# A hybrid attention and ConvFFN step on one core: the last two output tiles projected together, and split operands kept in memory between passes

## The chip, the cores and the metric

One core of a Trainium2 chip runs the whole step as one program. The metric is device time in microseconds (us) of one execution. TensorE (PE) does matrix products, VectorE (DVE), ScalarE (ACT) and GpSimd (POOL) do the elementwise work, SyncE (SP) issues all large transfers in program order, and 16 DMA engines carry them between memory (DRAM) and the on-chip buffers.

## The reference

The parts that the change touches, after attention and gated linear attention have made the mixed rows:

```python
def _conv_ffn(h, hist, p):
    L = h.shape[1]
    a, g = jnp.split(h @ p['w_up'], 2, axis=-1)
    a_ext = jnp.concatenate([hist.astype(a.dtype), a], axis=1)
    conv = p['b_conv']
    for j in range(CONV_W):
        conv = conv + p['w_conv'][j] * a_ext[:, j:j + L]
    y = (jax.nn.gelu(conv) * g) @ p['w_down']
    return y, a_ext[:, L:]
# per layer: x1 = x + gate * (mixed @ w_o);  h = rms(x1) modulated;  y = x1 + gate2 * conv_ffn(h)
```

There are 2048 prompt rows and 64 sample rows of width 1024; the FFN is 2816 wide, and w_up has 2 x 2816 columns. All arrays are float32.

## The kernel before

**Splits.** A float32 product is made of three faster products: each operand is split into a rounded part ("hi", a cast on ACT, L88) and the rest ("lo", a subtraction on DVE or POOL, L91). The up-projection of the FFN is done by a 2 x 2 block scheme with seven products, numbered m = 1, 6, 2, 5, 3, 7, 4 in the order in which they run. It needs eight combinations of the normed rows (the tile `comb`: four are written by ACT and DVE when the rows come back from a transpose, L1098 and L1100, four are sums on POOL, L1102 to L1105) and seven of the weights (`sraw`, L1181, then `wu` hi and lo).

**The output stage.** The 2112 rows are 17 tiles: 0 to 15 of 128 prompt rows, and 16 of 64 sample rows. `out_tile` is a generator with the steps: load and transpose the mixed rows `mx` (L1064), split them (`mT`), 48 matmuls with `w_o` (L96), gate and add the residual (`x1`, L1078 and L1079), store `x1`, norm it, transpose it (L1091), make `comb`, and then either split `comb` into the operands `h2` of pass 0 (tiles 0 to 5) or store it (tiles 6 to 16, `comb_d`, L1112: eight slots of 4 x 64 numbers for each of 128 partitions, thus 4096 pieces of 256 bytes). The loop around it runs the steps of neighbouring tiles side by side. `comb` has one buffer, so the next tile's L1100 waits until the store has landed. A scheduler orders each engine's instructions, each engine then runs its list in that order.

**The ConvFFN.** Three passes over the rows (tiles 0 to 5, 6 to 11, 12 to 16), 22 slots each, one per block of 128 FFN columns. A slot's PE work is the seven up products (L1287) and, between them, the down products of the slot before (L1467). All else in a slot is put in order by hand-written event times (`at(t, fn)`). In the last slot of passes 0 and 1 the operands of the next pass are fetched from `comb_d` (L1439, one transfer per product) and split again, hi on ACT (L1442), lo on DVE or POOL (L1446). The finished rows of a pass are gated on DVE (L1500), added to `x1` on POOL or DVE (L1505) and stored. `fst` is the buffer into which `w_up` and `w_down` are loaded. `conv_rows` loads and transposes the convolution's weights and history (L1196).

Of the kernel before, what the change touches and what calls it, by code (L numbers as in the profile page):

```python
# [11 lines left out]
F32 = mybir.dt.float32  # L12
F32R = mybir.dt.float32r
# [8 lines left out]
P = 128  # L22
D = 1024
# [38 lines left out]
def kernel(  # L62
# [51 lines left out]
    comb_d = [dr.tile([P, 8, 4, 64 * nt + 32 * smp], F32, tag=f"combd{t}", name=f"comb_d{t}") for t, nt, smp in PASSES[1:]]  # L114
# [138 lines left out]
    def norm_rows(pool, x, n, bufs=1):  # L253

        junk = pool.tile([P, D], BF16, tag="junk", name="junk", bufs=1)
# [4 lines left out]
        xn = pool.tile([P, D], F32, tag="xn", name="xn", bufs=bufs)  # L260
        V.tensor_scalar(xn[:n], x[:n], r[:n], None, op0=ALU.mult)
        return xn
# [786 lines left out]

    def out_tile(t, n, seq, src, pos0, tok0):  # L1050
# [24 lines left out]
        x1 = wk.tile([P, D], F32, tag="x1", name="x1", bufs=1)  # L1075
# [6 lines left out]
        xn = norm_rows(wk, x1, n)  # L1082
# [84 lines left out]
    def load_cols(c0, pool=None, bufs=4):  # L1167
# [32 lines left out]
    w0 = c6.enter_context(tc.tile_pool(name="w0", bufs=1, side="right", reuse_waits="tile"))  # L1200
# [4 lines left out]
    for t in range(len(tiles)):  # L1205
        g = outs[t]
        prev = outs[t - 1] if t else iter(())
        nxt = outs[t + 1] if t + 1 < len(tiles) else iter(())
        next(nxt, None)
        next(g, None)  # L1210
        if t == 0:
            next(g)
# [4 lines left out]
        next(prev, None)  # L1217
        next(prev, None)
        if t == len(tiles) - 1:
            next(g)  # L1220
            c6a.close()
            c4.close()
            fw = c7.enter_context(tc.tile_pool(name="fw", bufs=1, reuse_waits="tile"))
            raws.append({"a": load_cols(P), "g": load_cols(FF + P)})
            for m in (5, 6, 7, 3):
                block_sum(raws[0], m)
            w_f = {}
            for m, s in PRODUCTS:
                w_f[m] = two(f"wu{m}_")
                split(*w_f[m], block(raws[0], m), lo_eng=G if m in (3, 5, 6, 7) else V)  # L1230
        next(nxt, None)
        next(prev, None)

    with ExitStack() as c8:
        wk = c8.enter_context(tc.tile_pool(name="wk5", bufs=1, reuse_waits="tile"))
        ac = None

        def open_acc():
            nonlocal ac
            c6.close()  # L1240
            ac = c8.enter_context(tc.tile_pool(name="ac", bufs=1, reuse_waits="tile"))
# [25 lines left out]
        def slot(n, base, w, raw, raw_next, behind):  # L1267
# [111 lines left out]
            at(max(end[7] + 2.8, end[3] + 5.7), gated, 1, "m5", G)  # L1379
            at(end[4] + .1, add_bank, "b7")  # L1380
# [52 lines left out]
            if last_f and p + 1 < len(PASSES):  # L1433
                w1 = 64 * PASSES[p + 1][1] + 32 * PASSES[p + 1][2]
                there = base
# [12 lines left out]
                for m, s in PRODUCTS:  # L1448
                    there = max(there, end[m]) + 3.3
                    at(end[m] + .1, fetch, m, s)  # L1450
                    for i in range(2):
                        ks, eng = slice(2 * i, 2 * i + 2), G if m in (5, 6, 7) else V
                        at(there + 1.5 + i, half_hi, m, ks)
                        at(there + 2.6 + (2.0 if eng is G else 1.2) * i, half_lo, m, ks, eng)

            def down_tile(i, t):
# [4 lines left out]
                def products():  # L1461
                    if first_f:
                        acc[i] = ac.tile([P, D], F32, tag="acc", name="acc", bufs=8)
# [15 lines left out]

                at(t, products)  # L1480
                t += 6 * .232
                at(t + .1, add)
                if last_f:
# [3 lines left out]

                    def residual(c):
                        if c == 0 and i == nt:
                            g2[:] = [gate_rows(ac, 1, 1, "acc", 8)]  # L1490
                        elif c == 0 and n + 1 == NF and i == 0:
                            g2[:] = [gate_rows(ac, 1, 0, "gate")]
                        o["gate", i] = g2[0]
                        o["xs", i, c] = x = ac.tile([P, 512], F32, tag="xs", name="xs", bufs=2)
                        Q.dma_start(x[:rows_], x1_d[tile_ * P:tile_ * P + rows_, c * 512:(c + 1) * 512])
# [6 lines left out]
                    def finish_(c):  # L1502
                        cc = slice(c * 512, (c + 1) * 512)
                        a = o["acc", i][:rows_, cc]
                        (V if last and i % 2 else G).tensor_tensor(a, a, o["xs", i, c][:rows_], op=ALU.add)  # L1505
                        Q.dma_start((y_sample if i == nt else y_prompt[tile_ * P:tile_ * P + rows_])[:, cc], a)

                    for c in range(2):
                        at(t - 1.5 + c * .5 if last else late - 4 + c, residual, c)
                        at(t + 1.4 + c * .1 if last else late + 2.5 * c, gate_, c)  # L1510
                        at(t + 2.5 + c * .1 if last else late + 1 + 2.5 * c, finish_, c)
# [8 lines left out]
        at(.1, next, outs[-1])  # L1520
        at(7.5, next, outs[-1])
        at(13.0, open_acc)

        def conv_state():
            for s, dst in ((0, conv_prompt), (1, conv_sample)):
                pt = bank()
                T.transpose(pt[:2 * NF, :P], cout[s].rearrange("p j f -> p (j f)"), ident)
                ob = wk.tile([P, 768], F32, tag="cv", name="ob")
# [61 lines left out]
def _arrays(inputs):  # L1590
    out = {}
    for n, a in inputs.items():
        a = np.ascontiguousarray(np.asarray(a))
        if n in ("c_prompt", "c_sample") or (a.ndim == 2 and n not in ("c_prompt", "c_sample")):
            out[n] = a
        elif n in ("cache_ckv", "cache_kpe", "state_gla", "state_ffn_conv"):
# [13 lines left out]
```

## Time and profile before

| | us |
|---|---|
| three runs, median (lowest to highest) | 3171.83 (3169.92 to 3175.9) |
| the profiled execution | 3175.5 |
| its span in the trace | 3173.6 |
| PE busy in it | 3028.5 |
| DVE busy in it | 2479.6 |
| ACT busy, POOL busy in it | 1472.2, 1439.5 |

The span is from the first to the last instruction. The trace's times below count from the span's start. Attention fills the span up to about 1439, the output stage runs to about 1664, the FFN to the end.

### The profile page before, as it was taken

The numbers are of one execution on the slowest core, as the hardware profiler recorded it, in microseconds if no ns is written. First come the engines' busy times: TensorE is split into PE (matmuls) and PEld (weight loads), VectorE is DVE, ScalarE is ACT, GpSimd is POOL, SyncE is SP. The second block draws the span as 40 slices with busy tenths as digits, with TensorE's granted clock in tenths as the row PEclk, the third lists the DMA queues.
The fourth block names the chain that finished last, engine by engine and source line by source line (L and its number), as shares of the span: only waits on it lengthen the run. The fifth ranks groups of instructions, "written<-read, shape, count | busy, mean of one in ns | idle before, by whom it ended". The sixth has DMA issues, their size and how long they took to land. (4 is left out here: it accounts for less than half of the span.)

```text
span 3173.6 us, 46762 instructions
## 1 busy us (share of the span) xinstructions
PE 3028.5 (95%) x16730; PEld 2650.4 (84%) x16730; DVE 2479.6 (78%) x4617; ACT 1472.2 (46%) x3188; POOL 1439.5 (45%) x1170
## 2 busy tenths in 40 slices
PE   7999899999989999999998999999999999899996
PEld 4999788788758888887877999998899999789995
DVE  4766678778678888875546778788878778999997
ACT  4655433333247777773334434334434434444442
POOL 0233222212132222202336666666866665888884
PEclk9999899999979999999998999999999999999998
DMA  7544521111121112103574222223322222533232
GB/s 256 152 134 124 153 70 62 56 51 54 34 84 50 56 48 65 38 21 118 159 193 110 69 71 61 80 60 132 118 78 63 73 68 64 161 100 94 80 90 77
DMA packets 327641, 287.67 MB, mean 91 GB/s; under 512 B 104503, under 2 KB 272263, under 8 KB 327407
## 3 DMA queue, kind: packets, MB, share of 16 engines
q1 hardware_dynamic: 327407, 284.67, 30.4%
q8 instruction: 132, 2.16, 0.3%
q14 instruction: 102, 0.84, 0.1%
HBM read 217.63 MB, written 66.98 MB: 90 GB/s over the span
## 5 line engine op out<-in xcount | busy, mean ns | idle before, releaser
L1287 PE MATMUL bank<-h,wu 128*128 128x384 f32 (+1 forms) x5544 | 951.9, 326 | 38.3 <-ACT m L1306 35.3
L1287 PEld LDWEIGHTS bank<-h,wu 128*128 128x128 f32 x5544 | 917.9, 190 | 68.6 <-ACT m L1306 41.0
L1467 PE MATMUL bank<-wd,u 128*128 128x512 f32 (+1 forms) x2244 | 571.6, 398 | 5.4 <-DVE wd L1359 3.6
L1359 POOL TENSOR_TENSOR wu<-sraw,wu 128x512 fp32r<-128x512 f32 x252 | 365.4, 1450 | 347.0 <-ACT wu L1415 347.0
L1467 PEld LDWEIGHTS bank<-wd,u 128*128 128x128 f32 (+1 forms) x2244 | 411.9, 187 | 91.6 <-DVE wd L1359 5.1
L1478 DVE TENSOR_TENSOR acc<-acc,bank 128x512 f32<-128x512 f32 (+1 forms) x714 | 451.2, 678 | 41.2 <-PE bank L1467 38.3
L96 PE MATMUL bank<-w_g,hs 128*128 128x512 f32 (+4 forms) x1632 | 319.7, 347 | 0.0
L1359 DVE TENSOR_TENSOR wu<-fst,wu 128x512 fp32r<-128x512 f32 x189 | 215.6, 1166 | 93.6 <-ACT wu L1415 92.0
L96 PEld LDWEIGHTS bank<-w_g,hs 128*128 128x128 f32 (+1 forms) x1632 | 249.9, 188 | 33.3 <-issue 2.7
L91 DVE TENSOR_TENSOR pp<-bank,pp 128x512 fp32r<-128x512 f32 (+5 forms) x344 | 196.0, 577 | 38.2 <-ACT pp L88 33.7
L876 PE MATMUL bank<-pp,vv 128*128 128x512 f32 (+5 forms) x688 | 210.0, 392 | 13.0 <-DVE ob L900 6.7
L1345 DVE SCALAR_TENSOR_TENSOR cv<-a_sb,fcol,cv 128x768 f32<-128x768 f32 (+1 forms) x132 | 216.5, 1640 | 3.8 <-ACT cv L1341 1.5
L851 ACT ACTIVATE pr<-bank,mx 128x512 f32<-128x512 f32 (+4 forms) x328 | 204.7, 629 | 30.5 <-DVE mx L844 21.1
L88 ACT CAST pp<-bank 128x512 fp32r<-128x512 f32 (+5 forms) x344 | 170.0, 504 | 100.0 <-PE bank L863 95.9
L839 DVE TENSOR_REDUCE mx<-bank 128x1 f32<-128x512 f32 (+4 forms) x328 | 194.9, 599 | 24.4 <-PE bank L838 18.4
L96 PE MATMUL bank<-w_o,mT 128*128 128x512 f32 (+1 forms) x816 | 198.4, 400 | 1.4 <-ACT mT L88 0.9
L1312 POOL TENSOR_TENSOR m<-m,m 128x384 f32<-128x384 f32 (+1 forms) x132 | 173.6, 1315 | 42.4 <-ACT m L1306 35.3
L1415 ACT CAST wu<-sraw 128x512 fp32r<-128x512 f32 x252 | 154.9, 615 | 80.9 <-PE bank L1287 47.3
L96 PEld LDWEIGHTS bank<-w_o,mT 128*128 128x128 f32 (+1 forms) x816 | 148.8, 185 | 44.2 <-DVE mT L91 6.1
L863 PE MATMUL bank<-ident,pr 128*128 128x128 f32 (+1 forms) x1112 | 179.2, 276 | 3.8 <-DVE pp L91 2.9
L1181 POOL TENSOR_TENSOR sraw<-fst 128x512 f32<-128x512 f32 x128 | 181.7, 1420 | 0.0
L863 PEld LDWEIGHTS bank<-ident,pr 128*128 128x128 f32 (+1 forms) x1112 | 135.9, 141 | 39.9 <-DVE pp L91 9.3
(254 smaller groups left out, 5142.3 us busy)
## 6 DMA issues: line engine op xcount, KB each, us to landing
fst<-w_up SPq DMA_DIRECT2D x128, 512.0 KB
fst<-w_down SPq DMA_DIRECT2D x64, 512.0 KB
x<-x_prompt SPq DMA_DIRECT2D x32, 512.0 KB
ada_w<-w_ada SPq DMA_DIRECT2D x64, 256.0 KB
comb_d<-comb SPq DMA_DIRECT2D x10, 1024.0 KB
wst<-w_ada SPq DMA_DIRECT2D x16, 512.0 KB
hT_d<-hT SPq DMA_DIRECT2D x16, 512.0 KB
hT<-hT_d SPq DMA_DIRECT2D x16, 512.0 KB
```

What stands on the lines that cost most here:

```text
L91: (lo_eng or V).tensor_tensor(lo, src, hi.bitcast(F32), op=ALU.subtract)
L96: T.matmul(out, a, b, start=first and i == 0, stop=last and i == 2)
L839: V.reduce_max(mx[:qn, c:c + 1], po[:qn, :b - a], axis=AX.X)
L851: S.activation(pr[:qn, :b - a], box["s", i, j][:qn, :b - a], AF.Exp, bias=nb, accum_out=ls[:qn, i, j:j + 1])
L863: T.transpose(pt[:kn, i * qn:(i + 1) * qn], pr[:qn, j * P - a:j * P - a + kn], ident[:qn, :qn])
L876: T.matmul(box["o"][:, cs_], vv[:kn, key0 // P + j, :], pp[i][:kn, cs_], start=j == 0 and i == 0, stop=j == nk - 1 and i == 1)
L1181: G.tensor_tensor(s, x, y, op=op)
L1287: T.matmul(b[:, :cols_], w[m][i][:, k], h2[m][j][:, k, :cols_], start=first and k + i + j == 0, stop=k == 3 and i == 1, skip_group_check=n ...
L1345: V.scalar_tensor_tensor(v, o["a"][:, j:j + tot], col(j), v, op0=ALU.mult, op1=ALU.add)
L1359: eng.tensor_tensor(out[1], src, out[0].bitcast(F32), op=ALU.subtract)
L1467: T.matmul(po[c][:rows_], o["u"][a][:, c0:c0 + rows_], o["wd"][b][:, c * 512:(c + 1) * 512], start=a + b == 0, stop=a == 1)
L1478: V.tensor_tensor(x, x, y, op=ALU.add)
```

## The change

1. `conv_rows` moves from tile 4 to before the first projection, and uses buffers of `xn` and `comb`.
2. Tiles 15 and 16 are projected together (`project`), with the loop over `k` outside, so that each piece of `w_o` serves both.
3. Tiles 6 to 16 split `comb` in the output stage, and store seven hi and seven lo parts in three transfers (28, 8 and 20 times 64 numbers per partition: 7168 pieces of 256 bytes). The later passes fetch both parts, 14 transfers, and split nothing.
4. The first slot's `w_up` is no longer loaded three tiles ahead into a pool of its own, but after the last projection's place in the program. The host stores `w_up` by column block, so that a partition's piece is 4 KB long and not 512 bytes.
5. In the last slot the residual rows are loaded early, whole rows at a time, into free `fst` and `acc` buffers; nine of the ten final additions go to POOL; the convolution's state is written within the slot.
6. Smaller: the norm writes its square into `xn`, `x1` has two buffers, the accumulators lie in two pools.

```diff
     def out_tile(t, n, seq, src, pos0, tok0):
...
-        po = [bank(), bank()]
-        for k in range(KD):
-            for c in range(2):
-                mm3(po[c][:n], [mT[i][:, k, :n] for i in range(2)],
-                    [w_o[k][i][:, c * 512:(c + 1) * 512] for i in range(2)], k == 0, k == KD - 1)
+        mTs[t] = mT, n
         yield "proj"
+        po = pos.pop(t)
...
-            Q.dma_start(comb_d[p - 1][:, :, :, c0:c0 + hn], comb[:, :, :, :hn])
+            hi = wk.tile([P, 7, 4, 64], F32R, tag="hi", name="hi", bufs=1)
+            for m, s in PRODUCTS:
+                h, l = hi[:, s - (s > 2), :, :hn], c_(s)
+                split(h, l, l, lo_eng=G if m in (4, 5, 6, 7) else V)
+            dst = comb_d[p - 1]
+            Q.dma_start(dst[:, 0, :, :, c0:c0 + hn], hi[:, :, :, :hn].bitcast(F32))
+            Q.dma_start(dst[:, 1, 0:2, :, c0:c0 + hn], comb[:, 0:2, :, :hn])
+            Q.dma_start(dst[:, 1, 2:7, :, c0:c0 + hn], comb[:, 3:8, :, :hn])
         yield "done"
...
+    def project(*ts):
+        for t in ts:
+            pos[t] = [bank(), bank()]
+        for k in range(KD):
+            for t in ts:
+                mT, n = mTs[t]
+                for c in range(2):
+                    mm3(pos[t][c][:n], [mT[i][:, k, :n] for i in range(2)],
+                        [w_o[k][i][:, c * 512:(c + 1) * 512] for i in range(2)], k == 0, k == KD - 1)
...
-        s = (pool or fw).tile([P, KD, P], F32, tag="fst", name="fst", bufs=bufs)
-        Q.dma_start(s, w_up[:, c0:c0 + P].rearrange("(k p) f -> p k f", p=P))
+        s = fw.tile([P, KD, P], F32, tag="fst", name="fst", bufs=4)
+        Q.dma_start(s, w_up[c0 // P])
...
     next(outs[0])
-        if t == 4:
-            conv_rows(w0)
-        if t == len(tiles) - 4:
-            raws = [{"a": load_cols(0, w0, 2), "g": load_cols(FF, w0, 2)}]
+    conv_rows(wk4b)
+    for t in range(len(tiles) - 1):
+        g, nxt = outs[t], outs[t + 1]
+        last = t == len(tiles) - 2
+        next(nxt)
+        next(g)
+        if last:
+            next(outs[t - 1])
+            next(outs[t - 1])
+            next(nxt)
+            next(nxt)
+            project(t, t + 1)
+            next(outs[t - 1])
+        else:
+            project(t)
...
+    raws = [{"a": load_cols(i * P), "g": load_cols(FF + i * P)} for i in range(2)]
...
                 def fetch(m, s):
                     moving(m)
-                    Q.dma_start(h2[m][1].bitcast(F32)[:, :, :w1], comb_d[p][:, s])
-                def half_hi(m, ks):
-                    S.copy(h2[m][0][:, ks, :w1], h2[m][1].bitcast(F32)[:, ks, :w1])
-                def half_lo(m, ks, eng):
-                    h, l = h2[m][0][:, ks, :w1], h2[m][1][:, ks, :w1]
-                    eng.tensor_tensor(l, l.bitcast(F32), h.bitcast(F32), op=ALU.subtract)
+                    for i in range(2):
+                        Q.dma_start(h2[m][i].bitcast(F32)[:, :, :w1], comb_d[p][:, i, s - (s > 2)])
...
                     def residual(c):
...
-                        o["xs", i, c] = x = ac.tile([P, 512], F32, tag="xs", name="xs", bufs=2)
-                        Q.dma_start(x[:rows_], x1_d[tile_ * P:tile_ * P + rows_, c * 512:(c + 1) * 512])
+                        if not last:
+                            o["xs", i, c] = x = ac[1].tile([P, 512], F32, tag="xs", name="xs", bufs=2)
+                            Q.dma_start(x[:rows_], src[:, c * 512:(c + 1) * 512])
+                        elif c == 0:
+                            x = fw.tile([P, D], F32, tag="fst", name="fst", bufs=4) if i < 3 else acc_tile()
+                            Q.dma_start(x[:rows_], src)
+                            o["xs", i, 0], o["xs", i, 1] = x[:, :512], x[:, 512:]
...
-                        (V if last and i % 2 else G).tensor_tensor(a, a, o["xs", i, c][:rows_], op=ALU.add)
+                        (V if last and i == nt and c else G).tensor_tensor(a, a, o["xs", i, c][:rows_], op=ALU.add)
...
-                        at(t - 1.5 + c * .5 if last else late - 4 + c, residual, c)
+                        at(base + 8.0 + i if last else late - 4 + c, residual, c)
...
-        at(.1, next, outs[-1])
-        at(7.5, next, outs[-1])
+        at(8.0, next, outs[-2])
+        at(15.5, next, outs[-2])
+        at(17.0, next, outs[-1])
+        at(27.0, next, outs[-1])
```

Three places in the order of the engines' instructions follow. The first is PE at the start of the output stage; `mx` is tile 0's mixed rows, `fr` and `fh` the convolution's rows. Before:

```order
L1064 MATMUL bank_16938<-ident_66,mx_16699 128x128 x4
L1064 MATMUL bank_16945<-ident_66,mx_16699 128x128 x4
L96 MATMUL bank_16954<-w_o0_0_9755,mT0_16936 128x512
L96 MATMUL bank_16954<-w_o1_0_9756,mT0_16936 128x512
L96 MATMUL bank_16955<-w_o0_0_9755,mT0_16936 128x512
```

And after the change:

```order
L1080 MATMUL bank_16935<-ident_66,mx_16699 128x128 x4
L1080 MATMUL bank_16942<-ident_66,mx_16699 128x128 x4
L1216 MATMUL bank_16954<-ident_66,fr_16949 128x88
L1216 MATMUL bank_16957<-ident_66,fh_16952 128x44
L96 MATMUL bank_16962<-w_o0_0_9755,mT0_16933 128x512
```

The two transposes of `fr` and `fh` now stand between tile 0's transposes and its projection.

The second is DVE after the projection of tile 14, in the changed kernel; `x1_18744` is tile 14, `mT1_18686` tile 15, `comb_18453` tile 11 and `mT1_18762` tile 16. The last row is the input of the joint projection.

```order
L1091 TENSOR_TENSOR x1_18744<-bank_18620,gate_16929 128x512
L1091 TENSOR_TENSOR x1_18744<-bank_18621,gate_16929 128x512
L1092 TENSOR_TENSOR x1_18744<-x1_18744,x_18559 128x1024
L91 TENSOR_TENSOR mT1_18686<-bank_18687,mT0_18685 128x512
L91 TENSOR_TENSOR mT1_18686<-bank_18694,mT0_18685 128x512
L100 TENSOR_SCALAR ms_18753<-ss_18750 128x1
L265 TENSOR_SCALAR xn_18749<-x1_18744,r_18752 128x1024
L1113 TENSOR_SCALAR comb_18453<-bank_18454,mod_a1_123,mod_b1_125 128x2x64
L1113 TENSOR_SCALAR comb_18453<-bank_18463,mod_a1_123,mod_b1_125 128x2x64
L1113 TENSOR_SCALAR comb_18453<-bank_18454,mod_a1_123,mod_b1_125 128x2x64
L1113 TENSOR_SCALAR comb_18453<-bank_18463,mod_a1_123,mod_b1_125 128x2x64
L91 TENSOR_TENSOR mT1_18762<-bank_18763,mT0_18761 128x4x64
```

Tile 11's `comb` now stands ahead of tile 16's `mT`; before the change the `comb` there was tile 14's, and it stood behind.

The third is DVE in the first slot of the FFN; `comb_19133` and `comb_19220` are tiles 15 and 16 after the change, `wd1_19217` is the lo part of the first slot's `w_down`. Before (`comb_18969` is tile 16, `wd1_19093` the same `w_down`):

```order
L1309 TENSOR_TENSOR m1_18926<-m1_18926,bank_18913 128x384
L1359 TENSOR_TENSOR wu2_1_18966<-fst_18811,wu2_0_18965 128x512
L1100 TENSOR_SCALAR comb_18969<-bank_18970,mod_a1_123,mod_b1_125 128x2x32 x2
L1100 TENSOR_SCALAR comb_18969<-bank_18979,mod_a1_123,mod_b1_125 128x2x32 x2
L1329 TENSOR_TENSOR a_sb_18905<-m1_18926,bank_18949 128x6x64
L1333 COPY halo_18878<-a_sb_18905 128x2
L1345 SCALAR_TENSOR_TENSOR cv_19016<-a_sb_18905,fcol_16907,cv_19016 128x768 x2
L1309 TENSOR_TENSOR m1_18926<-m1_18926,bank_19019 128x384
L1352 TENSOR_TENSOR cv_19016<-cv_19016,m1_18926 128x6x64
L1317 MEMSET a_sb_19088 128x2
L1363 TENSOR_TENSOR u1_19086<-cv_19016,u0_19085 128x768
L1359 TENSOR_TENSOR wd1_19093<-fst_18911,wd0_19092 128x1024
```

And after the change:

```order
L1113 TENSOR_SCALAR comb_19133<-bank_19143,mod_a1_123,mod_b1_125 128x2x64 x2
L91 TENSOR_TENSOR comb_19133<-comb_19133,hi_19156 128x256 x3
L100 TENSOR_SCALAR ms_19183<-ss_19180 64x1
L265 TENSOR_SCALAR xn_19179<-x1_18923,r_19182 64x1024
L1341 TENSOR_TENSOR m1_19022<-m1_19022,bank_19099 128x384
L1384 TENSOR_TENSOR cv_19096<-cv_19096,m1_19022 128x6x64
L1349 MEMSET a_sb_19212 128x2
L1395 TENSOR_TENSOR u1_19210<-cv_19096,u0_19209 128x768
L1113 TENSOR_SCALAR comb_19220<-bank_19221,mod_a1_123,mod_b1_125 128x2x32 x2
L1113 TENSOR_SCALAR comb_19220<-bank_19230,mod_a1_123,mod_b1_125 128x2x32 x2
L91 TENSOR_TENSOR comb_19220<-comb_19220,hi_19243 128x4x32 x3
L1391 TENSOR_TENSOR wd1_19217<-fst_19007,wd0_19216 128x1024
```

In both, tile 16's `comb` stands ahead of the `w_down` split; after the change two `comb` tiles with their lo parts do, and tile 14's stands further up.

## Rows read from the trace of the kernel before

**Rows 1.** The page: busy time and share, and the chain that ended last.

```profile
PE 3028.5 (95%) x16730; PEld 2650.4 (84%) x16730; DVE 2479.6 (78%) x4617; ACT 1472.2 (46%) x3188; POOL 1439.5 (45%) x1170
...
PE bank L1287 26%; PE bank L1467 15%; DMA xs<-x_d 1%; DVE acc L1478 1%; POOL acc L1505 1%; DVE h L1446 0%; POOL sraw L1181 0%; DMA h<-comb_d 0%; DVE wu L1359 0%; DVE acc L1500 0%; POOL wu L1359 0%; POOL m L1312 0%; ACT wu L1415 0%; DVE cv L1345 0%; DVE wd L1359 0%
```

**Rows 2.** Timeline, start of the output stage: start, duration, engine, line, operation.

```profile
1440.91 11.51 PE L96 MATMUL bank<-w_o,mT 128*128 128x512 f32 x48 [0.24 <-ACT mT L88]
...
1443.02 0.38 SPq L1193 DMA_DIRECT2D fh<-state_ffn_conv  x1
```

**Rows 3.** Windows: busy by engine, granted clock, DMA share, GB/s.

```profile
1440.00:1446.50 6.50, 6.26 (x31) 4.98 (x29) 1.54 (x3) 1.07 (x2) 0.00 (x0) 1.00 0.72 224
...
1683.00:1697.00 14.00, 5.59 (x17) 5.59 (x18) 2.01 (x6) 3.09 (x7) 4.46 (x7) 0.52 0.55 98
```

**Rows 4.** Timeline of PE at the entry to the FFN.

```profile
1639.86 11.70 PE L96 MATMUL bank<-w_o,mT 128*128 128x512 f32 x48
...
1652.98 11.17 PE L96 MATMUL bank<-w_o,mT 128*64 128x512 f32 x48
...
1691.41 7.15 PE L1287 MATMUL bank<-h,wu 128*128 128x384 f32 x24 [11.26 <-ACT m L1306]
...
1710.26 1.56 PE L1467 MATMUL bank<-wd,u 128*128 128x512 f32 x6
...
1724.96 3.33 PE L1287 MATMUL bank<-h,wu 128*128 128x384 f32 x18
```

**Rows 5.** Timeline of DVE and POOL in a steady output tile.

```profile
1611.30 1.39 DVE L1078 TENSOR_TENSOR x<-bank,gate 128x512 f32<-128x512 f32 x2 [7.04 <-PE bank L96]
...
1615.07 0.72 DVE L1100 TENSOR_SCALAR comb<-bank,mod_a,mod_b 128x128 f32<-128x128 f32 x2
...
1616.72 0.74 DVE L261 TENSOR_SCALAR xn<-x,r 128x1024 f32<-128x1024 f32 x1
...
1619.53 0.74 POOL L1105 TENSOR_TENSOR comb<-comb 128x256 f32<-128x256 f32 x1
```

**Rows 6.** The store of comb: SP, DVE, DMA traffic 1621.4 to 1626.2.

```profile
1681.62 11.34 SPq L1112 DMA_DIRECT2D comb_d<-comb  x2
...
1688.23 0.34 DVE L1100 TENSOR_SCALAR comb<-bank,mod_a,mod_b 128x64 f32<-128x64 f32 x1 [6.09 <-DMA comb_d<-comb]
...
DMA packets 4001, 1.02 MB, mean 213 GB/s; under 512 B 4001, under 2 KB 4001, under 8 KB 4001
```

**Rows 7.** Tile h in the output stage: ns minimum, median, maximum.

```profile
L91 POOL TENSOR_TENSOR h<-comb,h x15: 733/916/926, 1487.5 to 1542.8; 128x256 fp32r<-128x256 f32 x15
```

**Rows 8.** Windows of six FFN slots around the first pass boundary.

```profile
2141.80:2165.00 23.20, 23.20 (x122) 21.54 (x120) 18.50 (x26) 9.35 (x16) 13.09 (x10) 1.00 0.23 69
...
2189.50:2220.00 30.50, 25.80 (x122) 22.78 (x121) 30.43 (x31) 11.82 (x19) 27.61 (x16) 0.94 0.22 70
...
sum 157.00, PE 144.63 PEld 131.58 DVE 135.36 ACT 66.19 POOL 116.71; mean PE 24.11 PEld 21.93 DVE 22.56 ACT 11.03 POOL 19.45
```

**Rows 9.** The same around the second boundary.

```profile
2793.90:2812.10 18.20, 18.20 (x115) 16.54 (x114) 17.66 (x28) 8.45 (x16) 14.82 (x13) 1.00 0.29 87
sum 142.20, PE 128.44 PEld 116.06 DVE 127.57 ACT 60.27 POOL 109.02; mean PE 21.41 PEld 19.34 DVE 21.26 ACT 10.04 POOL 18.17
```

**Rows 10.** Line L1446: ns minimum, median, maximum; a window of the fetches.

```profile
L1446 DVE TENSOR_TENSOR h<-h,h x16: 746/1218/2400, 2172.8 to 2730.2; 128x768 fp32r<-128x768 f32 x8, 128x576 fp32r<-128x576 f32 x8
L1446 POOL TENSOR_TENSOR h<-h,h x12: 1432/1862/2808, 2178.5 to 2721.9; 128x768 fp32r<-128x768 f32 x6, 128x576 fp32r<-128x576 f32 x6
...
2175.00:2180.00 5.00, 5.00 (x29) 4.73 (x28) 3.11 (x6) 2.39 (x3) 1.48 (x1) 1.00 1.05 363
```

**Rows 11.** Timeline of POOL at the end, and the chain there.

```profile
3145.92 1.29 POOL L1505 TENSOR_TENSOR acc<-acc,xs 128x512 f32<-128x512 f32 x1 [8.05 <-DVE acc L1500]
...
3169.10 1.25 POOL L1505 TENSOR_TENSOR acc<-acc,xs 64x512 f32<-64x512 f32 x1 [0.52 <-DMA xs<-x_d]
...
3156.54 3.75 DMA xs<-x_d
```

More of the change, by code (lines that the diff above doesn't have):

```diff
@@ L113 @@
     x1_d = dr.tile([TOK, D], F32, tag="x1d", name="x1_d")
-    comb_d = [dr.tile([P, 8, 4, 64 * nt + 32 * smp], F32, tag=f"combd{t}", name=f"comb_d{t}") for t, nt, smp in PASSES[1:]]
+    comb_d = [dr.tile([P, 2, 7, 4, 64 * nt + 32 * smp], F32, tag=f"combd{t}", name=f"comb_d{t}") for t, nt, smp in PASSES[1:]]
     gate_d = dr.tile([2, 2, D], F32, tag="gated", name="gate_d")
@@ L259, in norm_rows @@
         rsqrt(r[:n], ss[:n], 1.0 / D, EPS, n, 1)
-        xn = pool.tile([P, D], F32, tag="xn", name="xn", bufs=bufs)
+        if not in_place:
+            xn = pool.tile([P, D], F32, tag="xn", name="xn", bufs=bufs)
         V.tensor_scalar(xn[:n], x[:n], r[:n], None, op0=ALU.mult)
@@ L1081, in out_tile @@
         yield "res"
-        xn = norm_rows(wk, x1, n)
+        xn = norm_rows(wk, x1, n, in_place=True)
         yield "norm"
@@ L1204 @@
     next(outs[0])
[L1205 to L1212, printed above, removed]
-        if t == 4:
-            conv_rows(w0)
-        if t == len(tiles) - 4:
-            raws = [{"a": load_cols(0, w0, 2), "g": load_cols(FF, w0, 2)}]
[L1217 to L1232, printed above, removed]
+    conv_rows(wk4b)
@@ new lines @@
+    for t in range(len(tiles) - 1):
[10 more added lines that the diff above has]
+            next(outs[t - 1])
+        else:
+            project(t)
+            if t:
+                next(outs[t - 1])
+                next(outs[t - 1])
+            next(nxt)
+            if t:
+                next(outs[t - 1])
@@ L1234 @@
+    next(outs[-2])
+    next(outs[-1])
+    c6a.close()
+    c4.close()
+    fw = c7.enter_context(tc.tile_pool(name="fw", bufs=1, reuse_waits="tile"))
+    raws = [{"a": load_cols(i * P), "g": load_cols(FF + i * P)} for i in range(2)]
+    for m in (5, 6, 7, 3):
+        block_sum(raws[0], m)
+    w_f = {}
+    for m, s in PRODUCTS:
+        w_f[m] = two(f"wu{m}_")
+        split(*w_f[m], block(raws[0], m), lo_eng=G if m in (3, 5, 6, 7) else V)
     with ExitStack() as c8:
         wk = c8.enter_context(tc.tile_pool(name="wk5", bufs=1, reuse_waits="tile"))
-        ac = None
+        ac = [c8.enter_context(tc.tile_pool(name="ac0", bufs=1, reuse_waits="tile")), None]
+        n_acc = 0
@@ L1379, in slot @@
             at(max(end[7] + 2.8, end[3] + 5.7), gated, 1, "m5", G)
+            if n + 1 == len(steps):
+                at(end[3] + 3.0, lambda: conv_state())
             at(end[4] + .1, add_bank, "b7")
@@ L1462, in products @@
                     if first_f:
-                        acc[i] = ac.tile([P, D], F32, tag="acc", name="acc", bufs=8)
+                        acc[i] = acc_tile()
                     o["po", i] = po = [bank(), bank()]
@@ L1478, in add @@
                             V.tensor_tensor(x, x, y, op=ALU.add)
+                if n == 0 and i == 3:
+                    at(t - .01, open_acc)
                 at(t, products)
@@ L1486, in down_tile, with gate_load @@
                     late = o.setdefault("late", t) + 5.5 * i + 1.6
-                    def residual(c):
[L1489 to L1493, printed above, removed]
-                        o["xs", i, c] = x = ac.tile([P, 512], F32, tag="xs", name="xs", bufs=2)
-                        Q.dma_start(x[:rows_], x1_d[tile_ * P:tile_ * P + rows_, c * 512:(c + 1) * 512])
+                    def gate_load():
+                        if i in (0, nt) and (n + 1 == NF or i == nt):
+                            if i == nt:
+                                g2[:] = [acc_tile()]
+                            else:
+                                g2[:] = [ac[1].tile([P, D], F32, tag="gate", name="gate")]
+                            Q.dma_start(g2[0], gate_d[1, int(i == nt):int(i == nt) + 1].partition_broadcast(P))
+                        o["gate", i] = g2[0]
+                    def residual(c):
+                        if c == 0 or not last:
+                            gate_load()
+                        src = x1_d[tile_ * P:tile_ * P + rows_]
+                        if not last:
[5 more added lines that the diff above has]
+                            o["xs", i, 0], o["xs", i, 1] = x[:, :512], x[:, 512:]
                     def gate_(c):
@@ L1532 @@
         base += 4.0
-        for i, d in enumerate(behind):
-            if i == 2:
-                at(base + .01, conv_state)
+        for d in behind:
             base = d(base)
@@ L1595, in _arrays @@
             out[n] = a
+        elif n == "w_up":
+            out[n] = np.ascontiguousarray(a[0].reshape(KD, P, 2 * NF, P).transpose(2, 1, 0, 3))
         elif n in ("cache_ckv", "cache_kpe", "state_gla", "state_ffn_conv"):
```

34 lines of the change are left out of this document (16 added, 18 removed).

## The prediction

> **What bounds the kernel now.** I read the chain that ended last first: it is PE, 26% in the up products and 15% in the down products, and few waits for others [rows 1]. So only stretches in which PE waits can give something back, and only what makes PE wait can cost. The timeline of PE shows three such places, and the windows price them. The first is the entry to the FFN, where PE sat 11.26 us [rows 4] behind a DVE that waited 6.09 us for the store of `comb` [rows 6]. The second are the pass boundaries: six slots around the first take 157.0 us [rows 8]; a slot there is 23.2, so 157.0 - 6 x 23.2 = 17.8 us are lost. Around the second the six take 142.2 [rows 9]: two of 23.2, one between 18.2 and 23.2 (call it 19.6, for it has the long pass's down products and the short pass's up products) and three of 18.2 make 120.6, so about 21.6 us are lost. In the lossy slot DVE is busy 30.43 of 30.50 us and POOL 27.61 [rows 8]. The third is the end, where POOL's last addition starts at 3169.10, long after its first at 3145.92, because transfers into two small `xs` buffers alternate with additions [rows 11].
>
> **Part 1, `conv_rows`.** In the first place in the order, PE now needs `fh` before its first projection, which so far started at 1440.91 [rows 2]. `fh` is issued at 1443.02 [rows 2], last behind three loads of 512 KB. The window to 1446.5 moved 224 GB/s x 6.5 us = 1.46 MB [rows 3], a little less than those three (1.57 MB). So it lands near 1447, the transposes follow, and the projection starts near 1447.5: 6.6 us later, with nothing else for PE to do. If `fh`'s small pieces slip past the big loads it is 4. After idle PE runs at the lower level of its clock: after the 11.26 us, 24 matmuls took 7.15 us [rows 4], the granted clock there was 0.52 [rows 3], so near 1.2 GHz, while 18 later ones took 3.33 [rows 4], which is 4.44 for 24. That wait cost 2.7 us more; a shorter one costs between 0 and that, I take 1.4. Part 1: **+8** (4 to 9.5).
>
> **Parts 2 to 4, the entry.** A tile repeats every 13.2 us, nearly as from 1639.86 to 1652.98 [rows 4]. So DVE starts gating tile 14 two tiles after 1611.30 [rows 5], at 1637.7. From there to the end of the norm's `xn` (1617.46 - 1611.30) are 6.2 us [rows 5], of which `comb`'s two pieces are some 1.5 (the one shown is 0.72), so 4.7 without them. By the second place in the order, tile 11's `comb` (1.5) and tile 16's `mT` (1.3) follow before the joint projection may start. That is 1637.7 + 7.5 = 1645.2, with the hand-overs between engines 1646.5, against 1639.86 for tile 15 alone. The projection itself takes the same matmuls, 11.70 + 11.17 us [rows 4], plus 2.3 for the clock after some 6 us of idle: it ends near 1671.7, not at 1664.2. Then DVE gates tile 15 (1.4 + 1.2) and tile 16 (1.4), and copies tile 13's `comb` (1.5), before it may split the first slot's weights, since `w_up` is no longer loaded and summed ahead: `comb` 13 is done near 1678.5 and the first product runs near 1680.
>
> Now the chain of `comb`, which has one buffer. Before, a cycle is: first copy 1615.07 to last sum 1620.27, 5.2 us [rows 5]; then issue to landing 1688.23 - 1681.62 = 6.6 us [rows 6]; 11.8 in all, hidden under a 13.2 us tile. After, four lo parts follow on POOL, 0.92 each [rows 7], hence 3.6 us, for POOL does its sums first. The store grows from 4096 pieces of 256 bytes to 7168. 4001 pieces took 4.8 us with the DMA engines saturated [rows 6], which is 1.2 ns each. If the two first transfers are out before the last lo is done, only 2560 pieces are left (6.6 - 1.8 = 4.8 us to landing); if none is, 6.6 + 3.7 = 10.3. A cycle is thus 13.6 to 19.1 us; hi and lo are made side by side, so I take the middle, 16.3.
>
> The Trainium skill, DMA: Bandwidth & Descriptors, in Why small descriptors are slow (HBM only), charges a 256-byte piece 11 cycles for 8 of data, which with its ceiling of 435 GB/s would be an estimated 316 GB/s and 5.8 us for a store of 1.83 MB; its Specifications want pieces of 512 bytes or more for full rate, which speaks against this change. The row shows 213 GB/s and so 8.6 us, more than the cycle count makes; by the page's number three cycles would be some 8 us shorter.
>
> By the third place in the order, the first slot's `w_down` lo stands on DVE behind tiles 15 and 16, and those behind tile 14. From tile 13 to tile 16 are three cycles, 3 x 16.3 = 49 us: tile 16's `comb` is copied near 1727 (1719 to 1736), and the `w_down` split is done 3 us later, 1730. Before, that copy was at 1688.23 [rows 6]. PE's first down products wait for it; from the first down product to slot 2 were 1724.96 - 1710.26 = 14.7 us [rows 4]. So slot 2 starts near 1745 (1737 to 1754), 20 us later than before, and I add 2 for the clock after the idle: **+22** (8 to 32; the floor is what remains of the later joint projection if the store chain hides). In the tiles before, 16.3 exceeds 13.2 by 3, and the order lets `comb` fall up to three tiles behind; I take **+1.5** there.
>
> **Part 3, the boundaries.** The casts on ACT and the lo parts go: on DVE 8 x 1.22 = 9.8 us a boundary, on POOL 6 x 1.86 = 11.2 [rows 10]. The gating and the final additions stay, on the same two engines. At the first boundary slots of 23.2 leave DVE 4.7 us of room each (18.50 busy [rows 8]), so I take back 12 of 17.8. At the second DVE is busy 17.66 of 18.20 us [rows 9] and can't catch up, so only its own 9.8 come back: 10. Together **-22** (-8 to -39). What this adds is transfer: seven pairs of 1.57 MB. At the 363 GB/s seen when the DMA engines were full [rows 10] a pair takes 4.3 us. The seventh lands 30 us after the first fetch, but it is wanted a slot after its product, some 43 us after it, so they hide above 256 GB/s. The 4 KB pieces of `w_up` are hidden in the slots either way (DMA share 0.23 [rows 8]).
>
> **Part 5, the end.** Without waits for `xs`, POOL does nine additions of some 1.4 us (1.29 and 1.25 shown) from 3145.9 on: 12.6, so 3158.5 where it now ends at 3170.35 [rows 11]. **-12** (-6 to -14). Part 6 lies beside work that PE covers and I put it at 0 (half a microsecond a tile at the end of the norm at worst, under DVE's 7.04 idle [rows 5]).
>
> **The sum.** 8 + 22 + 1.5 - 22 - 12 = -2.5 us. The profiled execution's own time is 3175.5, its span 3173.6, and both stand a little above the median, 3171.8; I apply the sum to the median: 3169.
>
> **The rivals.** *The store chain hides* (0.32). If most of a store is out before the last lo, three cycles shrink by 8 us, and if DVE and ACT reach the `w_down` split between two of them the entry costs only its floor of 8. Then 8 + 8 - 22 - 12 = -18: 3154, and with both boundaries whole 3137. For it speaks that three transfers can start apart; against it that `w_down` stands behind tile 16 in a list that isn't reordered. *The store chain at its upper end* (0.27): 19.1 us a cycle, and ACT also waits for it before it can empty the second slot's first bank, so that four products (some 9 us) come after the wait instead of under it. The entry is then 22 + 8 + 9 = 39, the sum +14.5: 3186, slower. It decides at a cycle of about 17.5 us. Against it: tile 16 has half the data. *The boundaries give little* (0.10): gating and additions, not the splitting, hold PE there, and of 22 only 8 come back: +11.5, 3183. The forecast has 0.31.
>
> **Range and chances.** 0.2% is 6.3 us, about what a measurement of this kernel can tell from no change. The forecast's own range is 3163 to 3178. The first rival is faster, the second and third slower, a quarter of the forecast's range is faster: faster 0.40, within 0.2% 0.27, slower 0.33. For eight in ten I take 3146 to 3190.
>
> **What would show it.** Right: PE idle of 5 to 8 us before the first projection; the joint projection starting 5 to 8 us later than tile 15's did; DVE rows of `comb` that wait for `comb_d` in the first two slots, and PE waiting for `w_down` there; boundary windows with no rows of L1446 and with PE idle still, for gates or accumulators; POOL additions without gaps at the end. Wrong: slot 2 starting as early as 1725, a fetch that PE waits for, or an output tile longer than 14 us.

## The result and the profile after

The changed kernel takes 3202.81 us (median of six runs, 3198.52 to 3211.57) against 3173.76 (six runs of before, 3166.61 to 3179.69): ratio 1.0098, interval 1.0084 to 1.0112, so 27 to 36 us slower. My forecast of 3169 and its range up to 3190 were wrong.

The profiled execution has a span of 3209.8 us, 36.2 above the one of before. The attention stage, which the change leaves alone, ends anywhere from 1436 to 1448 us in the traces below. So traces are compared from tile 0's transposes of `mx` (1439.62 before, 1440.69 after) to the end: 1734.0 us before, 1769.1 after, **+35.1**. "Entry" below is from tile 15's `mx` transposes to the third slot: 86.8 us before (1638.20 to 1724.96), 130.1 after.

PE at the start of the output stage, after (it answers to [rows 2]):

```profile
1440.69 1.04 PE L1080 MATMUL bank<-ident,mx 128*128 128x128 f32 x8
1449.09 0.38 PE L1216 MATMUL bank<-ident,fr 88*128 88x88 f32 x1 [7.36 <-DMA fr<-b_conv]
1449.40 0.33 PE L1216 MATMUL bank<-ident,fh 44*128 44x44 f32 x1
1449.66 13.84 PE L96 MATMUL bank<-w_o,mT 128*128 128x512 f32 x48
```

PE waits 7.36 us for the small loads, and the projection behind it takes 13.84 us, not 11.51; the granted clock there is 0.81, against 1.00 before. PE at the entry, after (to [rows 4]):

```profile
1651.33 1.03 PE L1080 MATMUL bank<-ident,mx 128*128 128x128 f32 x8
...
1659.24 1.09 PE L1080 MATMUL bank<-ident,mx 64*128 64x64 f32 x8 [6.00 <-DMA mx<-mix_d]
1660.72 25.14 PE L96 MATMUL bank<-w_o,mT 128*128 128x512 f32 x96 [0.40 <-ACT comb L1111]
...
1695.84 4.30 PE L1319 MATMUL bank<-h,wu 128*128 128x384 f32 x12 [9.11 <-ACT wu L88]
1708.09 1.01 PE L1319 MATMUL bank<-h,wu 128*128 128x384 f32 x2 [7.95 <-ACT wu L88]
1712.33 8.65 PE L1319 MATMUL bank<-h,wu 128*128 128x384 f32 x34 [3.23 <-POOL wu L91]
...
1752.98 1.09 PE L1104 MATMUL bank<-ident,xn 64*128 64x64 f32 x8 [18.57 <-DVE xn L265]
...
1766.66 1.56 PE L1489 MATMUL bank<-wd,u 128*128 128x512 f32 x6
...
1781.40 8.61 PE L1319 MATMUL bank<-h,wu 128*128 128x384 f32 x48
```

The longest wait, 18.57 us, is for tile 16's `xn`. It looks like DVE's fault; DVE's own rows, the first copies into `comb` of tiles 8 to 16, say what DVE waited for:

```profile
1599.16 0.72 DVE L1113 TENSOR_SCALAR comb<-bank,mod_a,mod_b 128x128 f32<-128x128 f32 x2
...
1615.97 0.73 DVE L1113 TENSOR_SCALAR comb<-bank,mod_a,mod_b 128x128 f32<-128x128 f32 x2 [1.88 <-DMA comb_d<-comb]
...
1640.44 0.72 DVE L1113 TENSOR_SCALAR comb<-bank,mod_a,mod_b 128x128 f32<-128x128 f32 x2
...
1657.09 0.73 DVE L1113 TENSOR_SCALAR comb<-bank,mod_a,mod_b 128x128 f32<-128x128 f32 x2 [0.76 <-DMA comb_d<-comb]
...
1675.14 0.73 DVE L1113 TENSOR_SCALAR comb<-bank,mod_a,mod_b 128x128 f32<-128x128 f32 x2 [9.51 <-DMA comb_d<-comb]
...
1693.38 0.73 DVE L1113 TENSOR_SCALAR comb<-bank,mod_a,mod_b 128x128 f32<-128x128 f32 x2 [1.47 <-DMA comb_d<-comb]
...
1712.47 0.73 DVE L1113 TENSOR_SCALAR comb<-bank,mod_a,mod_b 128x128 f32<-128x128 f32 x2 [7.57 <-DMA comb_d<-comb]
...
1737.87 0.41 DVE L1113 TENSOR_SCALAR comb<-bank,mod_a,mod_b 128x128 f32<-128x128 f32 x1 [7.29 <-DMA comb_d<-comb]
...
1748.92 3.91 DVE L265 TENSOR_SCALAR xn<-x,r 64x1024 f32<-64x1024 f32 x1 [0.66 <-POOL r L101]
...
1755.72 0.34 DVE L1113 TENSOR_SCALAR comb<-bank,mod_a,mod_b 128x64 f32<-128x64 f32 x1
```

A cycle of `comb` goes from a tile's first copy to the next tile's. From tile 11 to tile 15 the cycles are 18.1, 18.2, 19.1 and 25.4 us, and each ends when a store has landed. In the tiles before, every second cycle ends so, and those took 16.8 us (1599.16 to 1615.97) and 16.7 (1640.44 to 1657.09); the one between, 24.5, ends with no wait. Of PE's 18.57 us some 3.5 lie before the landing at 1737.87; behind it, tile 15's `comb` with its lo parts and tile 16's norm still stood ahead of `xn`. The DMA traffic from 1666 to 1675, one whole tile's store (to [rows 6]):

```profile
DMA packets 7216, 1.84 MB, mean 204 GB/s; under 512 B 7216, under 2 KB 7216, under 8 KB 7216
```

It takes 9 us, nearly all behind the last lo part of tile 11. Windows of the two slots at the first boundary that still lose time, after (to [rows 8]):

```profile
2268.50:2296.20 27.70, 25.27 (x122) 22.90 (x121) 26.78 (x26) 12.26 (x24) 26.34 (x16) 0.94 0.56 175
2296.20:2324.00 27.80, 24.99 (x122) 23.04 (x121) 22.68 (x26) 10.82 (x20) 25.37 (x20) 0.94 0.34 111
```

In the first, DVE and POOL are nearly full again, in the second POOL is, without any splitting. Four slots from the last one of pass 0 took 110.6 us before and 101.9 after: 8.7 back. Before, the four slots started here, and the next one at 2275.58:

```profile
2165.00 8.61 PE L1287 MATMUL bank<-h,wu 128*128 128x384 f32 x48
...
2189.49 9.00 PE L1287 MATMUL bank<-h,wu 128*128 128x384 f32 x48
...
2219.99 8.61 PE L1287 MATMUL bank<-h,wu 128*128 128x384 f32 x48
...
2248.07 4.38 PE L1287 MATMUL bank<-h,wu 128*128 128x384 f32 x24
```

At the second boundary 100.9 (2693.06 to 2793.92) became 93.7: 7.2 back. The end, POOL and DVE after (to [rows 11]):

```profile
3189.41 1.29 POOL L1541 TENSOR_TENSOR acc<-acc,fst 128x512 f32<-128x512 f32 x1 [8.28 <-DVE acc L1536]
3191.51 6.34 POOL L1541 TENSOR_TENSOR acc<-acc,fst 128x512 f32<-128x512 f32 x4 [0.81 <-DVE acc L1536]
...
3200.08 5.17 POOL L1541 TENSOR_TENSOR acc<-acc 128x512 f32<-128x512 f32 x3
...
3204.16 1.63 DVE L1541 TENSOR_TENSOR acc<-acc 64x512 f32<-64x512 f32 x1
```

The last slot's first products, before and after:

```profile
3121.64 6.57 PE L1287 MATMUL bank<-h,wu 128*128 128x288 f32 x48
```

```profile
3163.93 6.57 PE L1319 MATMUL bank<-h,wu 128*128 128x288 f32 x48
```

From there to the end of the span are 45.9 us, against 52.0 before: 6.1 back.

### The profile page after: what moved, and what is told of

Read it like the earlier page. It is cut to its first block, busy times and chain, and to the rows that moved or that the text cites. A ratio compares the mean times of both kernels' runs of the same rounds, so it can differ in the third digit from the quotient of the medians.

```text
span 3209.8 us, 46980 instructions
## 1 busy us (share of the span) xinstructions
PE 3039.0 (95%) x16730; PEld 2657.7 (83%) x16730; DVE 2477.3 (77%) x4631; ACT 1480.7 (46%) x3237; POOL 1458.2 (45%) x1205
## 4 chain that ended last, share of the span: by engine, by line
PE 45%; DVE 7%; POOL 3%; issue 2%; DMA 1%; ACT 1%; SPq 0%; DVEq 0%; POOLq 0%; ACTq 0%
PE bank L1319 22%; PE bank L1489 13%; PE bank L96 6%; DVE acc L1500 2%; DVE wu L1391 1%; PE bank L880 1%; DVE cv L1377 1%; PE bank L867 1%; POOL sraw L1201 1%; DVE cv L1384 1%; DVE acc L1536 1%; POOL wu L1391 1%; POOL acc L1541 0%; PE bank L839 0%; DMA comb_d<-comb 0%
## 5 line engine op out<-in xcount | busy, mean ns | idle before, releaser
L843 DVE TENSOR_REDUCE mx<-bank 128x1 f32<-128x512 f32 (+4 forms) x328 | 195.1, 599 | 24.3 <-PE bank L842 18.3
```

The lines of the kernel that those rows point to most:

```text
L843: V.reduce_max(mx[:qn, c:c + 1], po[:qn, :b - a], axis=AX.X)
```

## The experiments

Theory A: the store chain of `comb`, one buffer and longer stores, lengthens the entry. Theory B: the weights that are no longer loaded ahead. Theory C: the joint projection. Runs of one execution are read by stage, from their traces; the totals of two traces can differ by some 2 us for no reason that was found. "Total" is from tile 0's transposes to the end of the span.

| run | entry | total |
|---|---|---|
| before / after | 86.8 / 130.1 | 1734.0 / 1769.1 |
| a_hi | 110.5 | 1744.4 |
| a_late | 117.0 | 1765.4 |
| a_sep | 130.7 | 1766.5 |
| b_nopre | 90.3 | 1739.6 |
| a_raw | 102.2 | 1736.0 |
| a_conv | 130.6 | 1760.1 |
| b_tail / b_up | 86.7 / 86.7 | 1730.2 / 1735.7 |
| x6 | 145.0 | 1773.3 |
| x5 | 89.3 | 1721.8 |
| a_nogate | 130.1 | 1744.3 |

**Only hi parts stored** (a_hi).

```diff
-            Q.dma_start(dst[:, 1, 0:2, :, c0:c0 + hn], comb[:, 0:2, :, :hn])
-            Q.dma_start(dst[:, 1, 2:7, :, c0:c0 + hn], comb[:, 3:8, :, :hn])
...
-                        Q.dma_start(h2[m][i].bitcast(F32)[:, :, :w1], comb_d[p][:, i, s - (s > 2)])
+                        Q.dma_start(h2[m][i].bitcast(F32)[:, :, :w1], comb_d[p][:, 0, s - (s > 2)])
```

> The changed kernel, but only the hi parts are stored (one transfer of 3584 pieces a tile in place of 7168), and the later passes fetch the hi parts twice; so the lo operands of passes 1 and 2 are not the real ones. The buffer of comb then waits for no store. The entry is counted from the end of tile 14's projection to the start of the third slot: 86.9 us before, 130.1 after. Theory A, the store chain of comb is what lengthens it: entry 95 to 110, no wait of DVE for comb_d. Theory B, the first slot's weights that are no longer loaded and summed ahead are what lengthens it: entry still 120 or more.

The entry fell by 19.6 us, to 110.5, half a microsecond above A's range and outside B's, and no row of DVE waits for `comb_d`. But 23.7 above before remain, with a wait for `xn` in them that no row puts down to a store:

```profile
1734.13 1.11 PE L1104 MATMUL bank<-ident,xn 64*128 64x64 f32 x8 [11.99 <-DVE xn L265]
```

**The last steps later** (a_late).

```diff
-        at(17.0, next, outs[-1])
-        at(27.0, next, outs[-1])
+        at(34.0, next, outs[-1])
+        at(43.0, next, outs[-1])
```

(tile 15's two steps went from 8.0 and 15.5 to 10.0 and 20.0.)

> The changed kernel with the last two tiles' norm and comb steps given later times in the first two slots, so that tile 16's transposes stand behind the second slot's products and its comb behind the first slot's w_down split. Theory A (waits for comb's stores block PE because of where these steps stand in the lists): PE's 18.6 us wait for xn goes, entry 108 to 118 us, the whole some 12 to 20 us faster than the change. Theory B (weights): the wait only moves to the next instruction that needs the weights, entry 125 or more.

The wait for `xn` is gone and the entry is 117.0, within A's range, but the whole gained only 3.7 of the 12 to 20 us. ACT and PE of that run show where the rest went:

```profile
1774.68 2.05 ACT L1498 COPY acc<-bank 128x512 f32<-128x512 f32 x4 [8.31 <-DMA comb_d<-comb]
```

```profile
1778.84 6.16 PE L1319 MATMUL bank<-h,wu 128*128 128x384 f32 x24 [9.76 <-ACT m L1338]
```

The accumulators of the first pass lie where `comb` and its neighbours lay, so ACT waits for tile 16's store, and PE for ACT. The chain has a second end; an order that lets PE pass the first only meets it there.

**Two projections again** (a_sep): `project(t, t + 1)` becomes two calls in the loop.

> The changed kernel, but tiles 15 and 16 projected one after the other as before. Theory C, the joint projection costs the entry its late start: PE's 6.0 us wait for mx and the half clock go, entry some 8 us shorter (122). Theory A: the store chain runs on at its own pace and sets the end, so the entry stays at 127 to 133; the wait only moves.

Entry 130.7: within A's range, and not C's 122. PE then waits longer for `xn`; what PE saves, the chain takes.

```profile
1756.10 1.08 PE L1104 MATMUL bank<-ident,xn 64*128 64x64 f32 x8 [33.45 <-DVE xn L265]
```

**Before, with late weights** (b_nopre).

```diff
-        if t == len(tiles) - 4:
-            raws = [{"a": load_cols(0, w0, 2), "g": load_cols(FF, w0, 2)}]
...
-            raws.append({"a": load_cols(P), "g": load_cols(FF + P)})
+            raws = [{"a": load_cols(i * P), "g": load_cols(FF + i * P)} for i in range(2)]
```

> The kernel before, but the first slot's w_up loaded only after the last projection, as the change does it. Theory B: PE waits some 15 to 20 us more at the first products, entry 100 to 107 instead of 86.9. Theory A: the weights are hidden behind the wait for comb's store that is there anyway (11.3 us), entry at most 92.

Entry 90.3, +3.5. PE waits for weights (7.4 and 4.8 us), but most of it lies inside the wait for `comb` that is there anyway: PE's wait for ACT's `m`, 11.26 us before, is 4.51 here. B alone falls.

**Stored unsplit** (a_raw): the casts, the lo parts and the hi store go; `comb` is stored once and fetched twice.

```diff
-            hi = wk.tile([P, 7, 4, 64], F32R, tag="hi", name="hi", bufs=1)
-            for m, s in PRODUCTS:
-                h, l = hi[:, s - (s > 2), :, :hn], c_(s)
-                split(h, l, l, lo_eng=G if m in (4, 5, 6, 7) else V)
...
+            Q.dma_start(dst[:, 0, 0:2, :, c0:c0 + hn], comb[:, 0:2, :, :hn])
+            Q.dma_start(dst[:, 0, 2:7, :, c0:c0 + hn], comb[:, 3:8, :, :hn])
```

> The changed kernel, but comb of tiles 6 to 16 is stored unsplit (3584 pieces, as before but for one slot that nobody reads), and the later passes fetch it twice without splitting it, so their operands are not the real ones. Joint projection, late w_up and early conv_rows stay. Theory A (splitting in the output stage and the longer store make the entry's 43 us): entry 90 to 98 us and no stalls in tiles 6 to 14. Theory B/C (late weights and joint projection make at least half of it): entry 108 or more. The boundaries, which fetch as much and split as little as the change, should stay as in the change.

102.2, between the two ranges: 27.9 of the 43.3 us are the split and its stores, 15.4 are the rest. Set beside a_hi, which splits but stores half, the stores of the lo parts make 19.6 of the 27.9, the casts and lo parts themselves 8.3. No projection in tiles 6 to 14 waits, and the boundaries stay (101.5 and 93.7 us); the two ranges for the entry do not hold. What makes the 15.4 is open. b_nopre's 3.5 for the late weights can't be subtracted, for there a wait for `comb` hid them; here PE waits 10.8 us for weights and 9.1 for `xn`. x5 below, with weights as late but the order of before, has an entry of 89.3, which speaks for the joint projection and the last tiles' steps inside the slots.

**`conv_rows` at tile 4** (a_conv): the call moves into the loop, its rows lie in `hi`.

> The changed kernel with conv_rows back at tile 4 (in the hi buffer, which is free there). If the load of fr and fh makes PE wait at the start of the output stage and nothing else covers it: PE's 7.4 us wait and the slow first projection go, 9 to 10 us from the first transposes to the third slot; rival: the store chain, which has its own pace from tile 6 on, takes back more than half of it.

From the first transposes to the third slot 9.4 us went, as expected (9.0 of the total), and the first projection starts 1.28 us after the transposes and takes 11.51. The entry, 130.6, takes back nothing.

**The end alone** (b_tail): part 5 on the kernel before.

> The kernel before with the change's part 5 alone (residual rows early, additions on POOL, the convolution's state in the last slot). From the last slot's first product to the end of the span: 51.8 us before, 45.9 in the change. If part 5 does this alone: 45 to 47, nothing else moves. My prediction had 12 us; that would be 40.

46.1 us from the last slot's first product to the end, as expected. My 12 was twice too large. The total fell by only 3.8, for the second boundary took 1.4 us more and the rest is spread.

**`w_up` by column block alone** (b_up).

```diff
-        Q.dma_start(s, w_up[:, c0:c0 + P].rearrange("(k p) f -> p k f", p=P))
+        Q.dma_start(s, w_up[c0 // P])
```

> The kernel before with w_up stored by column block on the host, nothing else. If its pieces of 512 bytes were hidden, as I held: no stage moves by more than 1 us. Rival: shorter transfers relieve the boundaries, where w_up queues with the fetches: 2 to 5 us less there.

The boundaries moved by -0.5 and 0.0: hidden, and the rival falls. The total moved by +1.7, of which 1.6 lie behind the last slot's first product, where no `w_up` is loaded any more; I can't explain them.

**Before's order, the split kept** (x6): a_sep and a_conv together, and `at(.1, ...)`, `at(7.5, ...)` for tile 16 as before.

> The changed kernel with conv_rows at tile 4, the last two tiles projected one by one, and the last tiles' norm and comb steps at the times that they had before; the split and the three stores stay, comb keeps its one buffer, w_up is still late. If the store chain sets the entry whatever the order around it: entry 110 to 125 us, with waits of DVE for comb_d. Rival, the new order (joint projection, tile 15 and 16 within the slots) made the loss: entry at most 98.

145.0 us, beyond both ranges, and the worst of all; the rival falls. PE there:

```profile
1687.66 3.57 PE L1315 MATMUL bank<-h,wu 128*128 128x384 f32 x10 [11.76 <-DVE wu L91]
...
1754.88 5.85 PE L1315 MATMUL bank<-h,wu 128*128 128x384 f32 x24 [52.77 <-ACT m L1334]
```

With tiles 15 and 16 ahead of all slot work, PE sits out three store cycles (19.3, 16.3 and 16.4 us) in one piece. So the change's later times had softened the chain, not caused it.

**A second `comb` buffer** (x5): only products 1, 2 and 3 are split ahead, which with a single `x1` makes room for it.

```diff
-        x1 = wk.tile([P, D], F32, tag="x1", name="x1", bufs=2)
+        x1 = wk.tile([P, D], F32, tag="x1", name="x1", bufs=1)
...
-        comb = wk.tile([P, 8, 4, 64], F32, tag="comb", name="comb", bufs=1)
+        comb = wk.tile([P, 8, 4, 64], F32, tag="comb", name="comb", bufs=2)
...
+            hi = wk.tile([P, 3, 4, 64], F32R, tag="hi", name="hi", bufs=1)
+            for i, m in enumerate(PRE):
+                split(hi[:, i, :, :hn], c_(dict(PRODUCTS)[m]), c_(dict(PRODUCTS)[m]), lo_eng=V)
```

> As the run above, but comb has two buffers; to make room only products 1, 2 and 3 are split in the output stage (1536 more pieces a tile, 5120 in all), the other four at the boundary as before, and x1 has one buffer. Store-chain theory: DVE no longer waits for comb_d, the entry falls to 87 to 95 us, the boundaries lose 8 to 12 us less than before in all, and the end is the change's: 8 to 14 us faster than the kernel before. Rival, the additional work of the split itself (casts, lo parts) costs the entry: 100 or more.

Entry 89.3, with no wait for `comb_d` left on DVE, and 12.2 us less than before in all. The boundaries gave 7.3 of it (four slots each: 106.0 and 98.1 us), a little under the expected 8 to 12. The order is that of x6, whose entry is 145.0. But against x6 it changes both the amount of splitting (and with it the store, 5120 pieces for 7168, in another order) and the buffer; how much of the 55.7 us is the buffer's isn't shown.

**No gating in passes 0 and 1** (a_nogate): `gate_` and `finish_` compute only in the last slot.

> The changed kernel without the gating and the residual addition of passes 0 and 1 (their rows are stored as they are, the output is not the real one). If gating on DVE and adding on POOL are what still holds PE at the boundaries: all slots there take 23.2, 19.6 and 18.2 us, and the 9.1 us and some 14 us that are lost there go to 3 or less together. Rival, the 14 fetches come late: they stay above 10.

All slots take 23.2, 19.6 and 18.2 us. The second of the two windows that answer to those above:

```profile
2289.60:2312.80 23.20, 23.20 (x122) 21.57 (x121) 17.39 (x23) 10.38 (x18) 14.39 (x12) 1.00 0.23 69
```

PE waits for nothing, while the 14 fetches are those of the change: they are not late.

**The best version, timed** (x5_timed), and **with the gating spread** (x8_spread).

```diff
-                    late = o.setdefault("late", t) + 5.5 * i + 1.6
+                    late = o.setdefault("late", t) + 7.2 * i + 1.6
```

> The version with two comb buffers and three products split ahead, timed. From its one look: 12 us less from the first transposes of the output stage to the end than the kernel before; 0.3 to 0.5% faster, interval clear of 1.

> As the run above, but the gating and additions of a finished pass are spaced 7.2 us a tile in place of 5.5. If they hold PE because they are crammed into two slots: 3 to 8 us less at the two boundaries. Rival: a later tile's accumulator is then late for the next pass, or the work only moves on: within 1 us or slower.

x5 takes 3162.75 us against 3174.79, ratio 0.9956 (0.994 to 0.9972): faster than the kernel before, as expected. The total of its trace here is 1722.8, 11.2 below before's. The spread version takes 3160.65, ratio 0.9949 (0.993 to 0.9968). Its first boundary is 3.3 us shorter (102.7 against 106.0). The second is 3.5 shorter over four slots, but the slot behind them is 4.3 longer, so there the work only moved on, as the rival had it. Together that is 2.5, a little under the expected 3 to 8, and the intervals of the two versions overlap, so its gain over x5 isn't shown.

## Why the prediction was wrong

The sum was right in its signs and wrong in its sizes. Measured, with the forecast in brackets: `conv_rows` +10.0 (+8): a start 7.7 us later and 2.3 for the slower projection; a_conv gave 9.0 of it back. Tiles 6 to 14 +3.0 (+1.5): three waits of 0.42 to 1.63 us for `mT`. Entry +43.3 (+22). Boundaries -15.9 (-22). End -6.1 (-12). That makes +34.3 of the +35.1. Of the 37.6 us between my sum of -2.5 and the trace, 21.3 are the entry's, 6.1 the boundaries', 5.9 the end's.

**The step that failed is the entry's term, and in it the cycle of `comb`.** I put it at 16.3 us, between 13.6 and 19.1, and counted three such cycles from tile 13 to tile 16, 49 us. In the output stage that was right: 16.7 and 16.8 us where a cycle ends with a store. In the slots it was not. There `comb`'s sums, casts and lo parts stand between the slot's own weight work on POOL and ACT. Tile 14's last cast comes at 1728.22, nearly 16 us after its first copy, and POOL's rows show what lies between (`wu` is the slot's weights):

```profile
1722.46 0.74 POOL L1116 TENSOR_TENSOR comb<-comb 128x256 f32<-128x256 f32 x1
...
1724.38 1.30 POOL L1391 TENSOR_TENSOR wu<-sraw,wu 128x512 fp32r<-128x512 f32 x1
1725.63 1.17 POOL L1118 TENSOR_TENSOR comb<-comb 128x256 f32<-128x256 f32 x1
1726.77 2.99 POOL L91 TENSOR_TENSOR comb<-comb,hi 128x256 f32<-128x256 f32 x3
1729.73 2.00 POOL L1391 TENSOR_TENSOR wu<-sraw,wu 128x512 fp32r<-128x512 f32 x1
1731.69 0.72 POOL L91 TENSOR_TENSOR comb<-comb,hi 128x256 f32<-128x256 f32 x1
```

The three cycles took 19.1, 25.4 and 17.9 us, 62.3 in all (in the last, tile 16's copy waited for no store). Of the first two, 12.8 and 19.9 us are the work up to the last lo part and only 6.3 and 5.5 the rest of the store: the store is not what grew. Tile 16's copy came at 1755.7, 104.4 us after tile 15's `mx` transposes, where I had some 89. From that copy to the third slot it was 25.7 us, where I had 20, for the wait did not stand where I put it: no row of PE waits for `w_down`; PE needs tile 16's transposes before the second slot's later products, so these came after the wait, not under it.

That is the outcome of the second rival, priced there at 39 us of entry, measured 43.3. It had 0.27; the cycle passed the point from which it was to decide. (With the third rival's 0.10 the chances add to 0.37 for slower, not to the 0.33 that I wrote.) But it named another stop for PE, a bank that ACT had not emptied; that form is x6's (52.77 us for ACT's `m`). a_hi, a_raw and x6 bear the chain out: with its extra stores and its splitting gone 27.9 of the 43.3 us go. For the other 15.4 the cause stays open; x5 fits, without telling the buffer from the smaller split. The joint projection's late start was right (PE at 1660.7, 9.4 us behind tile 15's `mx` transposes, as against my 8.3), though for the load of `mx`, which SP issues behind `comb`'s stores, and a_sep shows that it costs nothing while the chain ends last. The row had the store right, not the cycle count of the Trainium skill (DMA: Bandwidth & Descriptors, Why small descriptors are slow (HBM only)): 9 us, not the estimated 5.8.

**The boundaries** lose what I called the rest, gating and adding on engines that are full; a_nogate shows that this is all of it. The size was off because I let the first boundary regain what the removed work took. Against 23.2 us a slot, the four slots there lost 1.3, 7.3, 4.9 and 4.3 before, and lose 0, 0, 4.5 and 4.6 now. So only the first two, in which the splitting lay, gave their loss back; the time freed on DVE does not lie in the two where the gates and additions are crowded. At the second boundary it is the same: the second slot's 8.7 went, the two behind it lose 14.5, where they lost 13.0. The 15.9 lie between my 22 and the third rival's 8. That the fetches hide was right, and so was `w_up`.

**The end** was mis-sized first by the price of an addition: 1.4 us each from two rows of POOL working alone. Nine in a row, beside DVE's gates, took 15.8 us from the first start to the last end, 3.2 more than my 12.6. The rest of the miss lies around them: the first starts 25.5 us after the last slot's first product, 24.3 before, and 4.6 us follow the last, 3.3 before. DVE ends after POOL there (3205.8 and 3205.3), so POOL's price alone doesn't set the end.

## What to carry to other kernels

When a change makes a buffer's store longer, work out the buffer's whole cycle, from first write to landing, and compare it with the pitch of the loop: once it is longer, the tiles fall behind, and that falls due where the loop ends. Do not carry the cycle over to a stretch where other work stands between its steps: 16.7 us in the loop became up to 25.4 behind it. Another order only moves such a chain: the same steps in other orders gave entries of 117 to 145 us. A second buffer together with less splitting gave 89.

## What the hardware showed that I had not expected

The fetches ran faster than in the kernel before, where a full window had 363 GB/s [rows 10]. From 2226 to 2244 in the changed kernel:

```profile
DMA packets 1456, 7.46 MB, mean 414 GB/s; under 512 B 159, under 2 KB 159, under 8 KB 1455
```

Loads in pieces of some 5 KB moved at 414 GB/s, twice the rate of the stores in pieces of 256 bytes (204), with the DMA engines busy throughout in both (101 and 98%); whether the size of the piece or the direction makes the difference isn't shown. And DVE and POOL seem to stretch each other: a gate's product took 0.69 us on DVE with POOL at rest (at 2256.28), and up to 1.80 elsewhere; POOL's additions beside it took 1.3 to 2.0 us. No run tests that by itself.
